# A two-layer trunk kernel on one core: five early blocks per norm, another order of steps around each way down, the float32 copy of h on VectorE

## The chip, the cores and the metric

The kernel runs on one core of a Trainium2 chip, in one launch. The metric is device time in microseconds; the lower the better. The engines are TensorE (PE in the profile), VectorE (DVE), ScalarE (ACT), GpSimd (POOL) and SyncE (SP), which issues the transfers.

## The reference, cut to what matters

The input is x, 256 tokens of 2048 features, in float32. Two layers follow each other; in each, a modulated norm feeds a mixer and a second modulated norm feeds a feed-forward block (FFN) with a short causal convolution.

```python
mod = (c_act @ ada_w[i] + ada_b[i])[:, None, :]
sh1, sc1, g1, sh2, sc2, g2 = jnp.split(mod, 6, axis=-1)
h = rms_norm(x, norm_g[i, 0]) * (1.0 + sc1) + sh1
y = even_mixer(h, ...) if i % 2 == 0 else odd_mixer(h, ...)
x = x + g1 * y
h = rms_norm(x, norm_g[i, 1]) * (1.0 + sc2) + sh2
x = x + g2 * conv_ffn(h, ffn_w_up[i], ffn_conv_w[i], ffn_conv_b[i], ffn_w_down[i])

def conv_ffn(h, w_up, conv_w, conv_b, w_down):
    u = causal_dwconv(h @ w_up, conv_w, conv_b)      # width 3, per channel
    a, b = jnp.split(u, 2, axis=-1)                  # D_FF = 5632 each
    return (jax.nn.silu(a) * b) @ w_down
```

Layer 0 has the even mixer (a convolution module and sparse attention), layer 1 the odd one (sliding-window attention and a gated block).

## The kernel before, in words

**Tiling.** x is kept transposed in `xT`, 128 features on the partitions, 16 feature tiles (kt) and 256 tokens. A *block* is 128 output features over all kt. Weights stream from memory on SP's queue into raw tiles (`Weights.load_to`, three buffers). A piece is then split (`split_to`, L123 to L141): `whi` is the rounded part, made by ACT (L133), and `wlo` the rest, made by DVE, or by POOL for a share of them (L139, POOL only when `W.hold` is off). Three products per tile, high by high, high by low and low by high, give a float32 product. `mm_t` issues them: in layer 0 as three matmuls of 256 columns (L356 to L358, *unpaired*), in layer 1's FFN as one of 512 columns and one of 256 (L349 to L353, *paired*), after which `halves` folds the bank's two halves with an ACT copy (L689) and a DVE add (L690).

**The order.** The order on each engine is written by hand: what the Python code emits first stands first. `take()` (L319) hands out the next split piece, two ahead (AHEAD), and with it runs `advance()` (L281): one step of every chain in `steps`, and the start of one chain from `waiting` (two if more than two wait). A chain is a list of small steps, for example what follows an up block: fold, convolution (`conv`: ACT L666, DVE L667 and L668), silu or `gate` (DVE L673, then ACT L678 for the high part of g and DVE L679 for its low part). `tick()` emits `ada()` at a set rate: one DVE instruction over 128x2048 (L269), 192 in all, each making one column of the modulation; not while `W.hold`. `modulation()` emits missing columns on the spot.

**The norm stage.** Three of the four norms start with `Modulated.outer(n)`: before the norm's statistics are known, the first n blocks run over raw float32 weights (L360, two records per block and kt) against `hr`, which is x times the gain, with a 257th column for the shift (ACT L484 and L485, two kt ahead; DVE L472 for the gain `gs`). FIRST = 7 blocks in each FFN, FIRST_U = 6 in layer 1's mixer. At kt == STATS all chains are drained and `token_rstd` sums the squares (PE L443); at kt == STATS + SPREAD the result is spread (PE L419, DVE L454), and from there on the 16 tiles of h are made: DVE L529, ACT L531 (float32 copy `hf`) and L532 (high part), DVE L537 (low part). During these steps ada runs at the rate ADA_O. Then `W.hold` is set, so that no ada and no POOL split falls in, until four more blocks have run.

**The FFN.** Its 44 gates go in four quarters of QK = 11. In each, 22 up blocks run, then one more of the next quarter as cover (not in the last), then 16 down blocks over the 11 tiles of g, taken as pieces of five and six kt. `W.hold` is on from the quarter's last up block. `gated(k, q)` hands out g; before the last tile, k == 10 of the first down block, it calls `drain()`, which emits all that is left of every chain at once. "Turn" below means this passage from up to down.

Of the kernel before, what the change touches and what calls it, by code (L numbers as in the profile page):

```python
# [8 lines left out]
F32 = mybir.dt.float32  # L9
F32R = mybir.dt.float32r  # L10
I32 = mybir.dt.int32
AF = mybir.ActivationFunctionType
# [10 lines left out]
KF = FF // P  # L23
NQ = 4
QK = KF // NQ
FIRST = 7
FIRST_U = 6
HEADS = 8
NC = 15
L = 32  # L30
# [18 lines left out]
PER = 4  # L49
CAP = 4.0  # L50
LEAD = 4
STATS = 3
SPREAD = 2
ADA_O = 0.7
LO_A = 0.25
ADA_A = 0.25
CONV_A = 0
# [95 lines left out]
def trunk(ctx, tc, a, out):  # L153
# [134 lines left out]
    def advance():  # L288
        for s in list(steps):
            s.pop(0)()  # L290
        steps[:] = [s for s in steps if s]
        for _ in range(1 + (len(waiting) > 2)):
            if not waiting:
                break
            s = waiting.pop(0)
            s.pop(0)()
            if s:
                steps.append(s)
# [13 lines left out]
    def hook():  # L312
        for q in (hooks, beside):
            f = q.pop(0) if q else None
            if f:
                f()


    def take():  # L319
        w = W.take()  # L320
        advance()
        hook()
        tick()
        return w

    def drain():
        while steps or waiting:
            advance()
# [128 lines left out]
    class Modulated:  # L457
# [57 lines left out]
        def begin(self):  # L515
            kt = self.n
            self.n += 1
            gs, sh = self.gain(kt)
            t = sm.tile([P, T], F32, tag="hn", name="hn")
            if self.whole:  # L520
                if kt % 4 == 0:
                    self.tiles.append(hm.tile([P, 4, T], F32, tag="hm", name="hw"))
                V.tensor_tensor(t, xT[:, kt], self.bc, op=ALU.mult)
                S.activation(self.tiles[-1][:, kt % 4], t, AF.Identity, bias=sh, scale=gs)
                return
            if kt % 2 == 0:
                self.tiles.append(hm.tile([P, 2, 2, T], F32R, tag="hm", name="h"))
            h = self.tiles[-1][:, kt % 2]
            V.tensor_tensor(t, xT[:, kt], self.bc, op=ALU.mult)  # L529
            f = sm.tile([P, T], F32, tag="hf", name="hf")  # L530
            S.activation(f, t, AF.Identity, bias=sh, scale=gs)  # L531
            S.activation(h[:, 0], t, AF.Identity, bias=sh, scale=gs)  # L532
            self.open.append((h, f))

# [119 lines left out]
    def ffn(i, rest, last, split, up, down, share, pair):  # L654
        with tc.tile_pool(name=f"ffn{i}", bufs=2) as fp:
# [2 lines left out]
            h = Modulated(i, 1)  # L658
            out_rest(i, h, *rest)
            W.share = share  # L660
            half, gt = {}, {}

            def conv(o, jj, ab):
                w = fcw[:, jj + ab * KF]
# [6 lines left out]
            def gate(jj):  # L671
                y = half.pop((jj, 0))
                V.tensor_tensor(y, y, half.pop((jj, 1)), op=ALU.mult)  # L673
                q, j = divmod(jj, QK)
                if j % 2 == 0:
                    gt[q, j // 2] = fp.tile([P, 2, 2, T], F32R, tag="g", name="g", bufs=6)
                g = gt[q, j // 2][:, j % 2]
                steps.append([lambda: S.activation(g[:, 0], y, AF.Copy),  # L678
                              lambda: V.tensor_sub(g[:, 1], y, g[:, 0].bitcast(F32))])  # L679

            def gated(k, q):
                if k == QK - 1:
                    drain()
                    W.hold = False
                return gt[q, k // 2][:, k % 2]

# [5 lines left out]
            def follow(o, jj, ab, *before):  # L692
                if o.shape[-1] == 2 * T:
                    before = *before, *halves(o)
                    o = o[:, :T]
                if ab == 0:
                    waiting.append([*before, lambda: conv(o, jj, 0), lambda: S.activation(half[jj, 0], half[jj, 0], AF.Silu)])  # L697
                else:
                    waiting.append([*before, lambda: conv(o, jj, 1), lambda: gate(jj)])
# [18 lines left out]
            for q in range(NQ):  # L718
                if q:
                    rate["ada"] = up  # L720
                for b in range(2 * QK * q + (q > 0) if q else FIRST, min(2 * QK * (q + 1) + 1, 2 * KF)):
                    if q == 0 and b == FIRST + 4:
                        W.hold = False
                    if b == 2 * QK * (q + 1) - 1:
                        W.hold = True
                    follow(proj_t(h, pair=pair), b // 2, b % 2, *[lambda: None] * (2 if b == FIRST and b % 2 else 0))
                rate["ada"] = down
                end = q == NQ - 1
                for kt in range(KD):
                    if end and kt == KD - 2:  # L730
                        rate["ada"] = 0.0
                    if end and kt == KD - 1 and not last:
                        nxt = Modulated(i + 1, 0)
                        nxt.raw(0)
                    o = proj_t(lambda k: gated(k, q), QK, pair)
                    then = []
                    if end:
                        then = [lambda kt=kt: nc.sync.dma_start(last[:, kt], xT[:, kt])] if last else square_in(kt)
                    add_into_x(o, kt, i, 5, then)
# [881 lines left out]
```

## Time and profile before

| what | value |
|---|---|
| time, median of 3 runs | 2373.77 us (2373.11 to 2376.73) |
| the profiled execution | 2380.04 us, its span 2378.3 us |
| PE busy | 2288.6 us, 96% of the span, 14056 records |
| DVE busy | 1786.0 us, 75% |
| ACT busy | 1053.7 us, 44% |
| POOL busy | 379.4 us, 16%, all in the first 22 of 40 slices |
| transfers | 596.36 MB, mean 251 GB/s |
| mean granted clock of TensorE | 0.988 of full speed |

A record of a matmul in the timeline starts before the one ahead of it has ended, since matmuls are pipelined; the pace is read from start to start. "Idle before" is what the engine waited, and the name behind the arrow what ended it.

### The profile page before, as it was taken

What the parts mean: (1) busy time and instruction counts of PE and PEld (TensorE: products, weight loads), DVE (VectorE), ACT (ScalarE), POOL (GpSimd) and SP (SyncE); (2) the same over time, 40 slices, a digit from 0 to 9 for tenths busy, and PEclk for the clock granted to TensorE, in tenths of its full rate; (3) what the DMA queues carried; (4) which work ended last, traced back from release to release, by engine and by line L of the source; (5) the groups of instructions that cost most, each with busy time, mean ns of one, the idle gap of its engine ahead of it and who ended that gap; (6) DMA issues with size and microseconds to landing.
All of it is one profiled execution on the core that took longest, in us unless ns stands there. A gap on an engine that the chain in (4) does not pass through costs nothing. (4 is left out here: it accounts for less than half of the span.)

```text
span 2378.3 us, 36086 instructions
## 1 busy us (share of the span) xinstructions
PE 2288.6 (96%) x14056; PEld 2019.1 (85%) x14056; DVE 1786.0 (75%) x2827; ACT 1053.7 (44%) x1884; POOL 379.4 (16%) x238
## 2 busy tenths in 40 slices
PE   6898999999999999999999999999999999999999
PEld 3476677889999999999999777998788888888888
DVE  7758689747968878887986877667976766766765
ACT  2021254116444544544544556447544544554553
POOL 4233435101322222222222020000000000000000
PEclk9999999999999999999999999999999999999999
DMA  9968754776878878978887853556856546545545
GB/s 383 426 231 328 307 197 174 271 264 250 321 264 334 334 283 312 335 281 314 340 301 268 310 203 115 160 171 241 324 182 210 180 157 210 181 156 203 190 150 169
DMA packets 96365, 596.36 MB, mean 251 GB/s; under 512 B 11457, under 2 KB 14145, under 8 KB 44097
## 3 DMA queue, kind: packets, MB, share of 16 engines
q1 hardware_dynamic: 96194, 594.06, 68.4%
q8 instruction: 110, 1.80, 0.3%
q14 instruction: 61, 0.50, 0.1%
HBM read 591.92 MB, written 2.10 MB: 250 GB/s over the span
## 5 line engine op out<-in xcount | busy, mean ns | idle before, releaser
L133 ACT ACTIVATE whi<-raw 128x1024 fp32r<-128x1024 f32 (+2 forms) x659 | 626.8, 952 | 775.3 <-PE bank L357 352.3
L139 DVE TENSOR_TENSOR wlo<-raw,whi 128x1024 fp32r<-128x1024 f32 (+2 forms) x586 | 660.5, 1129 | 366.1 <-ACT whi L133 365.6
L269 DVE CUSTOM_DVE_ANT_0 ada<-ada,cB,adab 128x2048 f32<-128x2048 f32 x192 | 468.9, 2445 | 26.6 <-DMA ada<-adaw 26.0
L352 PE MATMUL bank<-h,whi 128*128 128x512 f32 x1215 | 432.6, 398 | 0.0
L358 PE MATMUL bank<-h,wlo 128*128 128x256 f32 x1328 | 377.3, 284 | 5.5 <-POOL wlo L139 4.9
L356 PE MATMUL bank<-h,whi 128*128 128x256 f32 x1328 | 377.1, 284 | 0.0
L357 PE MATMUL bank<-h,whi 128*128 128x256 f32 x1328 | 376.5, 284 | 0.0
L353 PE MATMUL bank<-h,wlo 128*128 128x256 f32 x1215 | 342.8, 282 | 5.5 <-DVE wlo L139 5.5
L139 POOL TENSOR_TENSOR wlo<-raw,whi 128x1024 fp32r<-128x1024 f32 (+2 forms) x73 | 192.1, 2634 | 667.4 <-ACT whi L133 601.3
L352 PEld LDWEIGHTS bank<-h,whi 128*128 128x128 f32 x1215 | 228.3, 188 | 51.3
L358 PEld LDWEIGHTS bank<-h,wlo 128*128 128x128 f32 x1328 | 255.6, 192 | 6.8 <-POOL wlo L139 5.7
L357 PEld LDWEIGHTS bank<-h,whi 128*128 128x128 f32 x1328 | 255.7, 193 | 0.0
L356 PEld LDWEIGHTS bank<-h,whi 128*128 128x128 f32 x1328 | 255.6, 192 | 0.0
L353 PEld LDWEIGHTS bank<-h,wlo 128*128 128x128 f32 x1215 | 229.4, 189 | 15.2 <-DVE wlo L139 12.0
L352 PE MATMUL bank<-g,whi 128*128 128x512 f32 x640 | 235.2, 407 | 0.9 <-DVE g L679 0.9
L357 PE MATMUL bank<-g,whi 128*128 128x256 f32 x704 | 199.6, 284 | 0.9 <-DVE g L679 0.9
L358 PE MATMUL bank<-g,wlo 128*128 128x256 f32 x704 | 200.1, 284 | 0.3
L356 PE MATMUL bank<-g,whi 128*128 128x256 f32 x704 | 199.3, 283 | 0.8 <-ACT g L678 0.8
L353 PE MATMUL bank<-g,wlo 128*128 128x256 f32 x640 | 182.7, 285 | 0.0
L360 PE MATMUL bank<-hw,raw 128*128 128x256 f32 x640 | 150.7, 390 | 14.1 <-DMA raw<-ev 9.5
L360 PEld LDWEIGHTS bank<-hw,raw 128*128 128x128 f32 x640 | 122.0, 195 | 43.4 <-issue 20.0
L352 PEld LDWEIGHTS bank<-g,whi 128*128 128x128 f32 x640 | 123.7, 193 | 28.7 <-ACT y L697 1.2
(281 smaller groups left out, 3696.9 us busy)
## 6 DMA issues: line engine op xcount, KB each, us to landing
ada<-adaw SPq DMA_DIRECT2D x192, 1024.0 KB, 6.1
raw<-wup SPq DMA_DIRECT2D x162, 1024.0 KB, 5.8
raw<-wdn SPq DMA_DIRECT2D x128, 704.0 KB, 4.2
raw<-out SPq DMA_DIRECT2D x44, 512.0 KB, 3.9
raw<-ev_a SPq DMA_DIRECT2D x16, 1024.0 KB, 4.9
raw<-ev SPq DMA_DIRECT2D x16, 896.0 KB, 14.7
raw<-wup SPq DMA_DIRECT2D x16, 896.0 KB, 4.7
raw<-cmp_w SPq DMA_DIRECT2D x8, 1024.0 KB, 8.5
```

What stands on the lines that cost most here:

```text
L133: nc.scalar.activation(hi[:, :n], raw, AF.Copy)
L139: eng.tensor_sub(lo[:, :n], raw, hi[:, :n].bitcast(F32))
L269: V.tensor_tensor_reduce(w, w, cB, 1.0, adab[:, i * 96 + j:i * 96 + j + 1], ALU.mult, ALU.add, m)
L352: PE.matmul(o, hi[:, s_], xx, start=start, stop=False)
L353: PE.matmul(o[:, :T], lo[:, s_], x[:, 0], start=False, stop=False)
L356: PE.matmul(o, hi[:, s_], x[:, 0], start=start, stop=False)
L357: PE.matmul(o, hi[:, s_], x[:, 1], start=False, stop=False)
L358: PE.matmul(o, lo[:, s_], x[:, 0], start=False, stop=stop)
L360: PE.matmul(o, w[:, s_], x, start=start, stop=stop)
```

## The change

FIRST and FIRST_U become 5, STATS 1 and ADA_O 0.3. `take()` runs `advance()` a second time while `W.hold` is on. The float32 copy of h is made by DVE in place of ACT. At the turn, not every chain is drained: `advance()` is called until the low part of the quarter's last gate has been emitted. The quarter's last up block is unpaired in layer 1's FFN too. Lines move by two behind L321 and by up to seven behind L678.

```diff
-FIRST = 7
-FIRST_U = 6
+FIRST = 5
+FIRST_U = 5
...
-STATS = 3
+STATS = 1
 SPREAD = 2
-ADA_O = 0.7
+ADA_O = 0.3
...
         w = W.take()
         advance()
+        if W.hold:
+            advance()
         hook()
         tick()
...
             f = sm.tile([P, T], F32, tag="hf", name="hf")
-            S.activation(f, t, AF.Identity, bias=sh, scale=gs)
+            V.tensor_scalar(f, t, gs, sh, op0=ALU.mult, op1=ALU.add)
             S.activation(h[:, 0], t, AF.Identity, bias=sh, scale=gs)
...
-            half, gt = {}, {}
+            half, gt, gates = {}, {}, set()
...
-                steps.append([lambda: S.activation(g[:, 0], y, AF.Copy),
-                              lambda: V.tensor_sub(g[:, 1], y, g[:, 0].bitcast(F32))])
+
+                def low():
+                    V.tensor_sub(g[:, 1], y, g[:, 0].bitcast(F32))
+                    gates.add(jj)
+
+                steps.append([lambda: S.activation(g[:, 0], y, AF.Copy), low])
...
                 if k == QK - 1:
-                    drain()
+                    while (q + 1) * QK - 1 not in gates:
+                        advance()
                     W.hold = False
...
-                    follow(proj_t(h, pair=pair), b // 2, b % 2, *[lambda: None] * (2 if b == FIRST and b % 2 else 0))
+                    last_up = b == 2 * QK * (q + 1) - 1
+                    follow(proj_t(h, pair=pair and not last_up), b // 2, b % 2, *[lambda: None] * (2 if b == FIRST and b % 2 else 0))
```

On DVE, at a turn of layer 1's FFN with a cover block, before the change, from the last gate but one (L673); L667 and L668 are a convolution, L690 a fold, L679 the low part of g:

```order
L673 TENSOR_TENSOR y<-y 128x256
L690 TENSOR_TENSOR bank<-bank,z 128x256
L139 TENSOR_TENSOR wlo<-raw,whi 128x640
L667 SCALAR_TENSOR_TENSOR y<-bank,fcw,y 128x255
L668 SCALAR_TENSOR_TENSOR y<-bank,fcw,y 128x254
L139 TENSOR_TENSOR wlo<-raw,whi 128x768
L679 TENSOR_TENSOR g<-y,g 128x256
L690 TENSOR_TENSOR bank<-bank,z 128x256
L139 TENSOR_TENSOR wlo<-raw,whi 128x640
L667 SCALAR_TENSOR_TENSOR y<-bank,fcw,y 128x255
L668 SCALAR_TENSOR_TENSOR y<-bank,fcw,y 128x254
L139 TENSOR_TENSOR wlo<-raw,whi 128x768
```

and directly behind these rows, still before, from the last gate (L673) to the first sum into x (L553):

```order
L673 TENSOR_TENSOR y<-y 128x256
L690 TENSOR_TENSOR bank<-bank,z 128x256
L667 SCALAR_TENSOR_TENSOR y<-bank,fcw,y 128x255
L668 SCALAR_TENSOR_TENSOR y<-bank,fcw,y 128x254
L679 TENSOR_TENSOR g<-y,g 128x256
L139 TENSOR_TENSOR wlo<-raw,whi 128x640
L553 SCALAR_TENSOR_TENSOR xT<-bank,mod,xT 128x256
```

The same place after the change (L675 is the gate, L682 the low part, L697 the fold, L669 and L670 the convolution):

```order
L669 SCALAR_TENSOR_TENSOR y<-bank,fcw,y 128x255
L670 SCALAR_TENSOR_TENSOR y<-bank,fcw,y 128x254
L675 TENSOR_TENSOR y<-y 128x256
L139 TENSOR_TENSOR wlo<-raw,whi 128x768
L682 TENSOR_TENSOR g<-y,g 128x256
L139 TENSOR_TENSOR wlo<-raw,whi 128x640
L697 TENSOR_TENSOR bank<-bank,z 128x256
L139 TENSOR_TENSOR wlo<-raw,whi 128x768
L669 SCALAR_TENSOR_TENSOR y<-bank,fcw,y 128x255
L670 SCALAR_TENSOR_TENSOR y<-bank,fcw,y 128x254
L139 TENSOR_TENSOR wlo<-raw,whi 128x640
L555 SCALAR_TENSOR_TENSOR xT<-bank,mod,xT 128x256
```

Before, the last up block's convolution stood behind the third of the down blocks' pieces (640, 768, 640), and its low part behind the fourth and the cover block's fold and convolution. Now the convolution stands behind the first piece, the low part behind the second, and the cover block's fold and convolution come after it.

On DVE, the end of layer 0's FFN norm stage before the change, the last three tiles of h made ahead of the first split piece (L472 is the gain, L529 and L537 the steps of h):

```order
L472 SCALAR_TENSOR_TENSOR gs<-mod,normg 128x1
L529 TENSOR_TENSOR hn<-xT,bc 128x256
L537 TENSOR_TENSOR h<-hf,h 128x256
L529 TENSOR_TENSOR hn<-xT,bc 128x256
L537 TENSOR_TENSOR h<-hf,h 128x256
L472 SCALAR_TENSOR_TENSOR gs<-mod,normg 128x1
L529 TENSOR_TENSOR hn<-xT,bc 128x256
L537 TENSOR_TENSOR h<-hf,h 128x256
L139 TENSOR_TENSOR wlo<-raw,whi 128x1024
```

and after it (L533 is the float32 copy on DVE, L531 and L539 the other two steps of h, L474 the gain, L269 ada):

```order
L474 SCALAR_TENSOR_TENSOR gs<-mod,normg 128x1
L531 TENSOR_TENSOR hn<-xT,bc 128x256
L533 TENSOR_SCALAR hf<-hn,gs,mod 128x256
L539 TENSOR_TENSOR h<-hf,h 128x256
L269 ISA ada,mod<-ada,cB,adab 128x2048
L269 ISA mod 128x1
L269 ISA ada,mod<-ada,cB,adab 128x2048
L269 ISA mod 128x1
L474 SCALAR_TENSOR_TENSOR gs<-mod,normg 128x1
L531 TENSOR_TENSOR hn<-xT,bc 128x256
L533 TENSOR_SCALAR hf<-hn,gs,mod 128x256
L539 TENSOR_TENSOR h<-hf,h 128x256
```

Four ada columns fall in this stage in both, but at the lower rate two of them are still missing when the last gain (L474) needs them, and are now emitted on the spot directly ahead of it. In layer 1's mixer three columns fall in the stage where five did, in layer 1's FFN two where four did; the rest moves into the up blocks that follow.

## Rows read from the trace of the kernel before

**Rows 1.** Waits of PE, whole span: in total us, times, longest us.

```profile
engine line waited for: us in total, times, longest us
...
PE bank L349 <- ACT g L678: 7.1, 4, 2.2
...
PE bank L353 <- DVE wlo L139: 5.5, 14, 1.0
...
PE bank L358 <- POOL wlo L139: 4.9, 4, 2.3
...
PE bank L350 <- DVE g L679: 2.0, 3, 0.7
...
PE bank L360 <- ACT hr L485: 1.6, 2, 1.1
...
PE bank L357 <- DVE mix L339: 1.4, 2, 0.7
...
PE bank L357 <- DVE g L679: 0.9, 3, 0.3
...
PE bank L356 <- ACT g L678: 0.8, 1, 0.8
```

**Rows 2.** Chain that ended last, by time, layer 1's FFN norm stage: start, us.

```profile
1590.22 9.10 PE bank L360 x42
...
1606.28 33.37 PE bank L360 x154
```

**Rows 3.** Timeline of PE in up blocks: start, us, form, [idle before <-releaser].

```profile
602.32 0.28 PE L358 MATMUL bank<-h,wlo 128*128 128x256 f32 x1
...
607.36 0.28 PE L358 MATMUL bank<-h,wlo 128*128 128x256 f32 x1
...
1760.00 0.40 PE L352 MATMUL bank<-g,whi 128*128 128x512 f32 x1
...
1762.12 0.28 PE L349 MATMUL bank<-g,wlo 128*128 128x256 f32 x1
```

**Rows 4.** Timeline of PE at the first down turn of layer 1's FFN.

```profile
1742.21 0.28 PE L353 MATMUL bank<-g,wlo 128*128 128x256 f32 x1
...
1744.11 0.38 PE L349 MATMUL bank<-g,wlo 128*128 128x256 f32 x1 [1.62 <-ACT g L678]
...
1745.17 0.63 PE L350 MATMUL bank<-g,whi 128*128 128x512 f32 x1 [0.68 <-DVE g L679]
```

**Rows 5.** Timeline of PE at the last turn of layer 1's FFN.

```profile
2308.45 0.28 PE L353 MATMUL bank<-g,wlo 128*128 128x256 f32 x1
...
2309.62 0.47 PE L352 MATMUL bank<-g,whi 128*128 128x512 f32 x1 [0.89 <-DVE g L679]
...
2309.92 0.28 PE L353 MATMUL bank<-g,wlo 128*128 128x256 f32 x1
...
2312.41 0.58 PE L349 MATMUL bank<-g,wlo 128*128 128x256 f32 x1 [2.21 <-ACT g L678]
```

**Rows 6.** Windows: length, busy us of PE, PEld, DVE, ACT, POOL, clock, DMA, GB/s.

```profile
1745.40:1748.80 3.40, 3.40 (x12) 2.81 (x12) 2.20 (x3) 0.74 (x1) 0.00 (x0) 0.50 0.04 14
...
2127.70:2131.10 3.40, 3.40 (x12) 2.92 (x12) 1.92 (x3) 1.01 (x2) 0.00 (x0) 0.50 0.02 5
...
2312.00:2318.80 6.80, 6.39 (x19) 5.36 (x20) 2.89 (x5) 1.93 (x3) 0.00 (x0) 0.50 0.03 11
...
1640.00:1742.00 102.00, 96.50 (x529) 79.66 (x529) 98.17 (x153) 62.20 (x105) 0.00 (x0) 1.00 0.76 275
```

**Rows 7.** Timeline of PE in layer 1's first norm stage.

```profile
1327.02 8.17 PE L360 MATMUL bank<-hr,raw 128*128 128x257 f32 x36 [1.11 <-ACT hr L485]
...
1335.66 4.60 PE L360 MATMUL bank<-hr,raw 128*128 128x257 f32 x20 [0.47 <-ACT hr L485]
```

**Rows 8.** DVE groups by form: count, busy us, mean ns, idle before.

```profile
L269 DVE CUSTOM_DVE_ANT_0 ada<-ada,cB,adab 128x2048 f32<-128x2048 f32 x192 | 468.9, 2445 | 26.6 <-DMA ada<-adaw 26.0
...
L673 DVE TENSOR_TENSOR y<-y 128x256 f32<-128x256 f32 x88 | 38.8, 441 | 0.0
...
L529 DVE TENSOR_TENSOR hn<-xT,bc 128x256 f32<-128x256 f32 x48 | 19.8, 419 | 0.1
...
L888 DVE TENSOR_SCALAR hs<-hs 30x256 f32<-30x256 f32 x2 | 0.8, 394 | 9.1 <-ACT hs L887 9.1
...
L954 DVE TENSOR_SCALAR cy<-xp,cvw 128x256 f32<-128x256 f32 x8 | 4.5, 560 | 0.1
```

**Rows 9.** Timelines of DVE and POOL, layer 0's first up blocks.

```profile
588.78 2.63 DVE L673 TENSOR_TENSOR y<-y 128x256 f32<-128x256 f32 x1
...
587.96 3.16 POOL L139 TENSOR_TENSOR wlo<-raw,whi 128x1024 fp32r<-128x1024 f32 x1 [25.49 <-ACT whi L133]
```

**Rows 10.** Timeline of DVE in layer 1's FFN norm stage.

```profile
1591.84 0.96 DVE L433 TENSOR_TENSOR sq<-sq 128x256 f32<-128x256 f32 x2 [0.63 <-ACT sq L429]
...
1599.70 0.16 DVE L445 TENSOR_SCALAR rv<-bank 128x2 f32<-128x2 f32 x1 [6.83 <-PE bank L443]
...
1602.08 0.48 DVE L418 TENSOR_SCALAR diag<-ident,rsy 128x128 f32<-128x128 f32 x2
```

## Prediction

> **What bounds the kernel now.** I read the page's busy shares first: PE is busy 96% of the span, so PE's own work, its waits and its clock are nearly all there is. Then the waits of PE [rows 1]: most of what is left after the start of the kernel stands at the turns of the FFNs (the waits for g) and where DVE or POOL have not split a weight in time (wlo). Then the chain that ended last, in a norm stage [rows 2]: it is PE over raw weights without a gap. Then PE's timeline at a turn [rows 4, 5] and the windows behind it [rows 6]: a turn costs twice, once as a wait and once as a spell at a granted clock of 0.50 (1.2 GHz in place of 2.4) that follows it. The sum is made against the profiled execution (2380.04 us, 6.3 above the median); the difference is put on the median, 2373.8. A measurement here can tell about 0.2%, or 4.7 us, from no change.
>
> **PE's own work.** A raw record takes 9.10/42 = 217 ns, so a block costs 434 ns per kt [rows 2]. Unpaired split work costs 5.04/14 = 360 ns per kt, paired work 2.12/6 = 353 ns [rows 3]. Blocks that move from raw to split therefore save 74 or 81 ns in each of 16 kt: two in layer 0's FFN (2.4 us), one in layer 1's mixer (1.2), two in layer 1's FFN (2.6), 6.2 together. Four last up blocks that become unpaired in layer 1 cost 4 x 16 x 7 ns = 0.5. Term A: **-5.7 us**, with hardly any doubt.
>
> **The turns.** In layer 1's FFN the first turn goes from 1742.21 to 1744.11 and on to 1745.17, where 0.12 us each would be the pace: 1.78 + 0.94 = 2.72 lost [rows 4]. Then comes a spell of 3.40 us at clock 0.50, which costs half of it, 1.7 [rows 6]. The waits count three such turns: four for the high part of g, 7.1 with a last one of 2.2 that is another place, three for the low part, 2.0 [rows 1]; the third has the same spell [rows 6]. 3 x 4.42 = 13.3. The last turn, without a cover block, loses 1.05 + 2.37 [rows 5] and a spell of 6.80 at 0.50, so 3.4 more [rows 6]: 6.8. What the change does there: with two steps per take under `W.hold` the last gate's chain is emitted over half as many pieces, it no longer lies behind the cover block's fold and convolution on DVE, and the unpaired last block needs no fold. The order shows the low part moved three positions of pieces forward. It now sits about one whole cover block ahead of its use, 16 x 353 ns = 5.6 us, against a lateness of 2.7; I take the three covered turns as free. The last turn has no cover; layer 0's last turn shows what an unpaired block leaves there, 0.8 for the high part [rows 1], and I leave 0.6 of it, without a spell. In layer 0 three waits of 0.3 and that one of 0.8 [rows 1] fall to 0 and 0.6, 1.1 gained (unpaired, no spell). Term B: -13.3 - 6.8 + 0.6 - 1.1 = **-20.6**. Ends: all waits stay half (+10), or the last turn is free too (-1.2). Late next at a turn is wlo of the second down piece, which the doubled steps now push behind a convolution (0.9 us of DVE): one of it is hidden by the two pieces split ahead.
>
> **The norm stages.** Three things change: PE's cover shrinks, DVE gets f, and ada moves.
> Statistics: in layer 1's FFN the squares are complete at 1592.80 [rows 10], 2.58 us after the raw work began at 1590.22 [rows 2]. Before, 3 kt of 7 blocks (9.1 us) covered that, now 1 kt of 5 blocks, 2.17. So 0.4 is lost there; from PE's sums to the diagonal it takes 1599.70 to 1602.56, 2.9 us [rows 10], against two kt of 4.34: no wait.
> Float32 copy: the trace has no such instruction on DVE. A one-source operation with scalars took 394 ns (30x256) and 560 (128x256, beside a busy POOL) [rows 8]; these are my ends, and I take the middle, 0.48. ACT gets 16 x 0.4 us back per norm, worth nothing, as it is not waited for there. The Trainium skill (VectorE: DVE Perf Modes, section "The perf-mode tier table") has this operation at twice the rate for float32 out of SBUF, 1227 ns for 2048 elements; as an estimate from that figure some 0.29 us for 256. By it the sum would be 3 us lower in layer 0's norm. The rows above speak against it, as none of the one-source rows of 256 is that short.
> DVE's load from the spread of the statistics to the end of the stage: 16 tiles x (0.42 + 0.42 + 0.48) = 21.1 us, plus ada at 2.45 [rows 8]; PE's time for it is 13 kt x 5 x 0.434 = 28.2 (before, 11 x 7 x 0.434 = 33.4, with 13.4 + 4 x 2.45).
> Layer 0's FFN: 21.1 + 4 x 2.45 = 30.9, so 2.7 too long (1.3 to 4.0 with f at its ends). Two of these ada are emitted on the spot just ahead of the last gain, one kt of 2.17 us before `hr` needs it; it shows as a wait for hr and then for the first split pieces. Behind it the two raw blocks fewer are made up by split ones, with POOL taking a share: one more wait like the four of 1.2 on average [rows 1]. One spell at half clock, 1.7 as at a turn. Together +5.6, ends 0 and 8.3 (4.0 + two POOL waits + 1.7).
> Layer 1's mixer: 21.1 + 3 x 2.45 = 28.5, level with 28.2. The two waits for hr there, 1.6 [rows 1, 7], come with ada in between and go, as two ada leave the stage. The third split block in place of the sixth raw one also covers one wait for mix, 0.7 [rows 1]: -2.3 (ends -2.3 and +1).
> Layer 1's FFN: 21.1 + 2 x 2.45 = 26.0, room enough. But in the up blocks behind it DVE is the bound: 98.17 of 102.00 us busy, PE 96.50 [rows 6], the 14 waits of 5.5 for wlo [rows 1]. Two more split blocks add 11.3 to PE and 4 x 1.2 to DVE, two more ada 4.9. Both get 10 to 11, so the waits stay about as they are. I take -1.0 for the convolutions that are spread over more PE time, +0.4 from above: -0.6, ends -4 (DVE catches up) and +3 (all ada in the way).
> Term C: +5.6 - 2.3 - 0.6 = **+2.7**.
>
> **Sum.** -5.7 - 20.6 + 2.7 = -23.6; 2373.8 - 23.6 = **2350**.
>
> **Rivals.**
> *The norms stay free.* DVE runs ahead of PE more than its load says, since it waits little before: layer 0's norm costs 0, layer 1's FFN gains 2, the turns are all free: -5.7 - 21.2 - 2.3 - 2 = -31.2, so 2342.6. For it speaks that DVE is idle at the end of the stages; against it the two ada on the spot.
> *The turn's wait only moves.* The doubled steps crowd DVE and ACT ahead of the down pieces' wlo, so that PE waits some 1.0 us for weights at each covered turn, with the spell of 1.7, and the last turn keeps half: the turns of layer 1 then give 3 x 1.7 + 3.4 = 8.5 in place of 19.5, so 2361. For it: the same DVE work is only put in another order, and spells follow such waits. Against it: two pieces are split ahead, and no other wait lies at the turns now.
> *DVE becomes the bound in all three norms.* It decides where f takes over (28.2 - 4.9)/16 - 0.84 = 0.62 us. At 0.85, DVE falls 16 x 0.23 = 3.7 behind in each, PE stalls in most kt, and spells as after the last turn follow twice (6.8 at half, 3.4 each): 10.5 per norm, 31.5 in all, with the gain in the mixer's norm gone. -5.7 - 20.6 + 31.5 = +5.2, so 2379, slower. For it: a DVE instruction with two SBUF sources (L673, 0.44 us on average, [rows 8]) took 2.63 us while POOL split a weight from 587.96 on for 3.16 [rows 9]; f beside POOL could do the same. Against it: POOL splits nothing in these stages and is idle in layer 1. The Trainium skill (SBUF — State Buffer, section "Who interferes with whom") says that such a VectorE instruction, or one in a two-port mode, and GpSimd lock each other out for a whole instruction; the trace agrees with its 2.63 us.
> *The change does not do what it says:* the order shows each part in place, so this has no chance of its own.
>
> **How the numbers follow.** Forecast 0.53 (2344 to 2357), norms free 0.2, wait moves 0.22, DVE bound 0.03, none of these 0.02. The range 2339 to 2363 holds the first three nearly whole with their unknown costs. Faster by over 0.2% (under 2369.0): all of the first two, most of the third: 0.93; the same 0.04; slower 0.03.
>
> **What would show it.** In the changed profile the waits for g in layer 1's FFN are gone but for the last quarter, and the windows behind the three covered turns have clock 1.00. PE's busy time falls by 5.7 and by the spells, some 13 us in all. In layer 0's norm stage there is a wait for hr or wlo of one to three microseconds, behind two ada in a row. f takes 0.39 to 0.56 us. Wrong it would be if the waits for wlo grow by over 5 us at the turns, or if PE waits for h or hr in layer 1's norms.

## The result and the profile after

The changed kernel takes 2349.71 us (median of 4 runs, 2348.95 to 2351.11), the kernel before 2374.27 on the same occasion: a ratio of 0.9887, 95% interval 0.9875 to 0.9899. That is 26.9 us less by the ratio, 24.6 by the medians; forecast were 2350 and a gain of 23.6. The profiled execution took 2349.61 us.

The page's span and busy times:

```profile
span 2347.9 us, 36331 instructions
...
PE 2266.1 (97%) x14168; PEld 2007.7 (86%) x14168; DVE 1810.3 (77%) x2872; ACT 1043.4 (44%) x1840; POOL 383.2 (16%) x239
```

PE is busy 22.5 us less than in the first trace of before, and 14.8 less than in the second (2280.9; first experiment). Within their spans the clock stood at 0.50 for 56.1 and 39.2 us in those two, and for 23.9 here. Half of the differences, 16.1 and 7.7, is what half clock costs; it leaves 6.4 and 7.1 for saved work, near the 5.7 of the sum. The "some 13 us in all" of the prediction is near the fall against the second trace, and well short of that against the first.

The waits of PE, in total us, times and longest, the lines that answer to [rows 1]:

```profile
PE bank L355 <- DVE wlo L139: 4.5, 11, 1.1
...
PE bank L360 <- POOL wlo L139: 4.5, 8, 0.9
...
PE bank L360 <- DVE wlo L139: 2.1, 3, 1.0
...
PE bank L358 <- ACT whi L133: 0.6, 1, 0.6
...
PE bank L362 <- ACT hr L487: 0.5, 1, 0.5
...
PE bank L352 <- DVE g L682: 0.4, 1, 0.4
...
PE bank L359 <- DVE g L682: 0.4, 1, 0.4
```

The waits for g are down from 11.7 us (7.1 + 2.0 + 0.9 + 0.8, and the 0.89 of [rows 5]) to 0.8, those for hr from 1.6 to 0.5. Those for split weights stay: before, wlo cost 4.9 from POOL and 0.5 from DVE in unpaired blocks and 5.5 in paired ones, now 4.5 + 2.1 and 4.5; a wait for whi of 0.6 is new.

PE's timeline at the first turn of layer 1's FFN, the place of [rows 4]:

```profile
1729.51 0.28 PE L355 MATMUL bank<-g,wlo 128*128 128x256 f32 x1
1729.63 0.28 PE L351 MATMUL bank<-g,wlo 128*128 128x256 f32 x1
1729.75 0.40 PE L352 MATMUL bank<-g,whi 128*128 128x512 f32 x1
```

No gap is left where 1.62 and 0.68 us stood. And at the last turn, the place of [rows 5]:

```profile
2284.20 0.28 PE L355 MATMUL bank<-g,wlo 128*128 128x256 f32 x1
2284.61 0.39 PE L351 MATMUL bank<-g,wlo 128*128 128x256 f32 x1
2285.36 0.51 PE L352 MATMUL bank<-g,whi 128*128 128x512 f32 x1 [0.37 <-DVE g L682]
```

From 2284.20 to 2285.36 there are 1.16 us for two steps of 0.12: 0.9 is lost, where it was 3.4. Windows behind the first, the second, the third and the last turn (length, then busy us of PE, PEld, DVE, ACT, POOL, the clock, the DMA share, GB/s):

```profile
1736.80:1740.20 3.40, 3.40 (x20) 2.99 (x21) 3.17 (x6) 0.74 (x1) 0.00 (x0) 1.00 0.69 225
...
1917.20:1920.60 3.40, 3.40 (x21) 2.93 (x20) 2.19 (x6) 1.82 (x3) 0.00 (x0) 1.00 0.58 210
2103.60:2107.00 3.40, 3.40 (x21) 2.93 (x20) 2.19 (x6) 1.83 (x3) 0.00 (x0) 1.00 0.56 210
2285.60:2289.00 3.40, 3.40 (x20) 2.97 (x20) 1.75 (x3) 1.59 (x2) 0.00 (x0) 1.00 0.62 217
```

The clock is 1.00 in all four; before, it was 0.50 behind the first, the third and the last [rows 6].

Where the time went is best read by stretches, from the start of PE's first record of one stage to that of the next, in its timeline. The up blocks and the ways down come out the same within 0.2 us from trace to trace unless a spell at half clock falls into them, and so does layer 1's FFN norm (145.5 to 145.7 in three traces of the same code), so they tell more than a kernel's whole time. The other stretches vary more, with no edit in them: the start took 508.7 to 516.1 us over all traces of this document, layer 1's mixer 286.5 to 290.3 in six traces of the same code, layer 0's FFN norm 144.8, 146.2 and 146.0 in three. One trace can't tell a difference of 2 us there. The kernel before was profiled a second time (first experiment), and the table has both.

| stretch | before | before, again | after |
|---|---|---|---|
| start to layer 0's FFN norm | 513.0 | 512.3 | 512.2 |
| layer 0's FFN norm to its first way down | 146.7 | 145.9 | 144.8 |
| its four ways down (each up to the next up block or norm) | 258.5 | 258.5 | 257.2 |
| its other up blocks | 378.0 | 377.9 | 377.9 |
| layer 1's mixer, norm and all | 293.8 | 293.3 | 288.1 |
| layer 1's FFN norm to its first way down | 148.7 | 148.4 | 145.5 |
| its first three ways down | 199.2 | 197.7 | 187.7 |
| its other up blocks | 367.4 | 367.3 | 367.6 |
| its last way down and the end | 72.9 | 71.8 | 67.0 |

The end of layer 0's norm stage is where the sum expected the change to cost. DVE and, below it, POOL in the changed kernel:

```profile
540.96 2.35 DVE L269 CUSTOM_DVE_ANT_0 ada<-ada,cB,adab 128x2048 f32<-128x2048 f32 x1
...
543.23 2.35 DVE L269 CUSTOM_DVE_ANT_0 ada<-ada,cB,adab 128x2048 f32<-128x2048 f32 x1
...
545.50 0.16 DVE L474 SCALAR_TENSOR_TENSOR gs<-mod,normg 128x1 f32<-128x1 f32 x1
...
548.80 2.06 DVE L139 TENSOR_TENSOR wlo<-raw,whi 128x1024 fp32r<-128x1024 f32 x1 [2.02 <-ACT whi L133]
```

```profile
547.40 2.37 POOL L139 TENSOR_TENSOR wlo<-raw,whi 128x1024 fp32r<-128x1024 f32 x1 [118.32 <-ACT whi L133]
```

Two ada stand ahead of the last gain, as the order showed; then DVE's first weight split takes 2.06 us, 1.2 being usual, beside POOL's, which started first and ended at 549.77: from there on it took 1.1. On PE this comes to five short waits, none with a spell behind it:

```profile
546.43 2.43 PE L362 MATMUL bank<-hr,raw 128*128 128x257 f32 x10 [0.53 <-ACT hr L487]
...
549.83 0.39 PE L360 MATMUL bank<-h,wlo 128*128 128x256 f32 x1 [0.73 <-POOL wlo L139]
...
560.09 0.38 PE L360 MATMUL bank<-h,wlo 128*128 128x256 f32 x1 [1.02 <-DVE wlo L139]
...
563.60 0.39 PE L358 MATMUL bank<-h,whi 128*128 128x256 f32 x1 [0.62 <-ACT whi L133]
...
564.86 0.39 PE L360 MATMUL bank<-h,wlo 128*128 128x256 f32 x1 [0.76 <-DVE wlo L139]
```

The float32 copy on DVE takes 0.413 us each (count, busy us, mean ns, idle before):

```profile
L533 DVE TENSOR_SCALAR hf<-hn,gs,mod 128x256 f32<-128x256 f32 x48 | 19.8, 413 | 1.7
```

### The profile page after: what moved, and what is told of

Same layout as the page of the kernel before. It is cut to its first block, busy times and chain, and to the rows that moved or that the text cites. A ratio compares the mean times of both kernels' runs of the same rounds, so it can differ in the third digit from the quotient of the medians.

```text
span 2347.9 us, 36331 instructions
## 1 busy us (share of the span) xinstructions
PE 2266.1 (97%) x14168; PEld 2007.7 (86%) x14168; DVE 1810.3 (77%) x2872; ACT 1043.4 (44%) x1840; POOL 383.2 (16%) x239
## 3 DMA queue, kind: packets, MB, share of 16 engines
q1 hardware_dynamic: 96914, 594.06, 68.6%
## 4 chain that ended last, share of the span: by engine, by line
PE 77%; DVE 13%; DMA 5%; issue 2%; ACT 2%; POOL 2%; SPq 0%; DVEq 0%; ACTq 0%; POOLq 0%
PE bank L354 15%; PE bank L360 11%; PE bank L359 11%; PE bank L358 11%; PE bank L362 10%; PE bank L355 8%; DVE ada L269 4%; DMA raw<-ev 2%; DVE wlo L139 2%; PE bank L373 1%; PE bank L370 1%; PE bank L371 1%; PE bank L369 1%; PE bank L352 1%; POOL wlo L139 1%
## 5 line engine op out<-in xcount | busy, mean ns | idle before, releaser
L133 ACT ACTIVATE whi<-raw 128x1024 fp32r<-128x1024 f32 (+2 forms) x669 | 637.1, 953 | 763.9 <-PE bank L359 357.9
L139 DVE TENSOR_TENSOR wlo<-raw,whi 128x1024 fp32r<-128x1024 f32 (+2 forms) x595 | 674.1, 1135 | 355.6 <-ACT whi L133 350.6
L269 DVE CUSTOM_DVE_ANT_0 ada<-ada,cB,adab 128x2048 f32<-128x2048 f32 x192 | 476.7, 2486 | 27.2 <-DMA ada<-adaw 26.4
L354 PE MATMUL bank<-h,whi 128*128 128x512 f32 x1185 | 421.9, 398 | 0.8 <-ACT whi L133 0.8
L360 PE MATMUL bank<-h,wlo 128*128 128x256 f32 x1440 | 408.4, 284 | 5.5 <-POOL wlo L139 3.4
L358 PE MATMUL bank<-h,whi 128*128 128x256 f32 x1440 | 408.1, 283 | 0.6 <-ACT whi L133 0.6
L359 PE MATMUL bank<-h,whi 128*128 128x256 f32 x1440 | 407.4, 283 | 0.0
L355 PE MATMUL bank<-h,wlo 128*128 128x256 f32 x1185 | 333.8, 282 | 3.6 <-DVE wlo L139 3.5
L360 PEld LDWEIGHTS bank<-h,wlo 128*128 128x128 f32 x1440 | 276.3, 192 | 7.2 <-POOL wlo L139 4.2
L358 PEld LDWEIGHTS bank<-h,whi 128*128 128x128 f32 x1440 | 276.3, 192 | 0.9 <-ACT whi L133 0.8
L359 PEld LDWEIGHTS bank<-h,whi 128*128 128x128 f32 x1440 | 276.3, 192 | 0.2
L354 PEld LDWEIGHTS bank<-h,whi 128*128 128x128 f32 x1185 | 222.6, 188 | 51.4 <-ACT whi L133 1.1
L355 PEld LDWEIGHTS bank<-h,wlo 128*128 128x128 f32 x1185 | 223.7, 189 | 11.2 <-DVE wlo L139 7.7
L354 PE MATMUL bank<-g,whi 128*128 128x512 f32 x640 | 228.6, 398 | 0.0
L358 PE MATMUL bank<-g,whi 128*128 128x256 f32 x704 | 199.2, 283 | 0.0
## 6 DMA issues: line engine op xcount, KB each, us to landing
raw<-ev SPq DMA_DIRECT2D x16, 896.0 KB, 14.7
```

What stands on the lines that cost most here:

```text
L133: nc.scalar.activation(hi[:, :n], raw, AF.Copy)
L139: eng.tensor_sub(lo[:, :n], raw, hi[:, :n].bitcast(F32))
L269: V.tensor_tensor_reduce(w, w, cB, 1.0, adab[:, i * 96 + j:i * 96 + j + 1], ALU.mult, ALU.add, m)
L354: PE.matmul(o, hi[:, s_], xx, start=start, stop=False)
L355: PE.matmul(o[:, :T], lo[:, s_], x[:, 0], start=False, stop=False)
L358: PE.matmul(o, hi[:, s_], x[:, 0], start=start, stop=False)
```

## The experiments

Each kernel was profiled; where a median with an interval is given it was also timed against the kernel before. Stretches are those of the table.

**The kernel before, once more** (no edit).

> The kernel before, profiled once more. If the 6.3 us by which the first profiled execution stood over the median were chance of that one execution, this one stands within 3 us of 2374, and the stretches of the two traces show in which part of the program the difference lies. If the profile itself costs those 6 us, this one comes out near 2380 again.

It took 2374.75, with a span of 2373.0. So the first execution was long by chance, and the place of most of it is seen: 0.7 in the stretch up to layer 0's FFN norm, 0.8 in that norm's stretch, 1.5 and 1.1 at the last two turns of layer 1's FFN. PE at the third of them, and windows behind the first and the third:

```profile
2122.90 0.38 PE L349 MATMUL bank<-g,wlo 128*128 128x256 f32 x1 [1.62 <-ACT g L678]
...
2123.97 0.50 PE L350 MATMUL bank<-g,whi 128*128 128x512 f32 x1 [0.68 <-DVE g L679]
```

```profile
1743.00:1746.40 3.40, 3.40 (x13) 2.83 (x11) 2.39 (x3) 1.14 (x2) 0.00 (x0) 0.55 0.06 22
...
2124.30:2127.70 3.40, 3.40 (x20) 2.94 (x19) 1.88 (x3) 1.59 (x2) 0.00 (x0) 1.00 0.07 23
```

The waits before it are the same 1.62 and 0.68 us as at the first turn, but the clock behind is 1.00 here, and 0.50 at the same place in the first trace [rows 6]. A wait of this size does not always bring a spell.

**The part for the turns alone**, in the kernel before:

```diff
         advance()
+        if W.hold:
+            advance()
...
-                    drain()
+                    while (q + 1) * QK - 1 not in gates:
+                        advance()
...
-                    follow(proj_t(h, pair=pair), ...
+                    follow(proj_t(h, pair=pair and not last_up), ...
```

> The kernel before with the part for the turns alone (two steps per take under hold, only the last gate waited for, last up block unpaired). Theory (the turns give nearly all of the gain): term B and the unpaired blocks, -20.6 + 0.5, so about 2354, and no spell at half clock behind the three covered turns of layer 1's FFN. Rival (the turn's wait only moves, and the norms gave the rest): 2362 to 2366, with new waits for wlo at the turns.

2362.09 us against 2376.16, ratio 0.9941 [0.9929, 0.9954]: a gain of 14 us, between the theory's 20 and the rival's 8 to 12. The turns did what the theory says: ways down of layer 1's FFN of 63.6, 62.1, 62.1 and 67.3 us, no spell behind them, no wait for g left but 0.37 at the last; at the first, 0.23 and 0.70 for wlo. But the stretches ahead of the first ways down grew to 148.1 us in layer 0 and 150.4 in layer 1. Some 1.7 of each is spells (6.8 us at half clock in layer 0's, where before had 3.4, and 3.4 in layer 1's, where before had none), and PE has new waits there (in total us, times, longest):

```profile
PE bank L354 <- ACT whi L133: 1.8, 1, 1.8
...
PE bank L358 <- ACT whi L133: 1.5, 1, 1.5
```

**The norms alone**, in the kernel before:

```diff
-FIRST = 7
-FIRST_U = 6
-STATS = 3
-ADA_O = 0.7
+FIRST = 5
+FIRST_U = 5
+STATS = 1
+ADA_O = 0.3
```

> The kernel before with five early blocks, STATS 1 and ADA_O 0.3 alone; the float32 copy stays on ScalarE. Theory (PE's saved work comes through, and VectorE has room without the copy): -6.2 of PE work, -2.3 in layer 1's mixer, -1 in layer 1's FFN, +1.5 for the two ada on the spot in layer 0: 2366. Rival (ScalarE, with the copy on it, can't keep up over the shorter stage): waits for h, hr or whi at the end of each norm stage, 3 us or more each, so 2372 or slower.

2369.87 us, ratio 0.9975 [0.9966, 0.9985]: 6 us, some 2 short of the theory's 8. Layer 1 took 289.2 and 146.6 us in its mixer and in its FFN's first stretch, 6.3 less than before where the theory has 7.1. Layer 0's stretch took 149.7, 3 more than before, with two spells of 3.4 us at half clock where before had one. It has a wait for whi from ACT, as the rival says, and one of 2.0 us for wlo, at the place of the 2.3 of [rows 1]:

```profile
PE bank L358 <- DVE wlo L139: 2.7, 2, 2.0
...
PE bank L356 <- ACT whi L133: 1.6, 1, 1.6
```

**The copy alone**, in the kernel before:

```diff
-            S.activation(f, t, AF.Identity, bias=sh, scale=gs)
+            V.tensor_scalar(f, t, gs, sh, op0=ALU.mult, op1=ALU.add)
```

> The kernel before with the float32 copy of h on VectorE alone. Theory (seven raw blocks cover it: VectorE's load with the copy at 0.41 us is 29.8 us against 33.4): no difference, 2372 to 2376. Rival (ScalarE was what ended the norm stages late, and the copy's move frees it): 1 to 4 us faster, 2370 to 2373, with the waits for hr in layer 1's mixer gone.

2376.28 against 2376.16, ratio 1.0 [0.9991, 1.0009]: nothing, as the theory has it. By stretches it is two things that offset each other: layer 0's got 1.4 longer than the mean of before (147.8, in this trace without a spell), layer 1's 2.0 shorter (146.5). So even with seven blocks the copy's place matters in layer 1's FFN norm; it is the whole that comes to nothing. The three parts apart come to 14 + 6 + 0 = 20 us; the whole gave 26.9 by its ratio.

**The change with the copy back on ACT** (the last diff, the other way round).

> The changed kernel with the float32 copy of h back on ScalarE. The parts measured apart (turns 14, norms 6, copy 0) add to less than the whole (about 26). Theory (the copy's move is worth something only with five blocks: ScalarE, with hr, whi and two copies of h to make, is what the shorter norm stage of layer 0 waits for): 4 to 6 us slower than the changed kernel, nearly all of it between the start of layer 0's norm stage and its first way down (144.8 us in the changed kernel, about 149.5 here). Rival of the prediction (VectorE is the one short of time there, so the copy costs): 1 to 3 us faster than the changed kernel.

2357.21 us, ratio 0.9924 [0.9912, 0.9937], against 0.9887 for the change: 7.5 us slower by the medians, 8.8 by the ratios. So the copy's move is worth nothing on the whole with seven blocks and about a third of the gain with five. By stretches, layer 0's took 147.0 (144.8), the mixer 289.8 (288.1), layer 1's 148.9 (145.5). The theory had nearly all of it in layer 0; only layer 1's 3.4 is clear of what the same code gives from trace to trace, and 1.7 of it is a spell at half clock. The waits of PE for hr, whi and wlo grew by 4.4 us in all, among them:

```profile
PE bank L355 <- DVE wlo L139: 5.9, 12, 1.1
...
PE bank L358 <- ACT whi L133: 1.5, 2, 0.8
...
PE bank L362 <- ACT hr L487: 0.8, 1, 0.8
```

That ACT is what is late shows on DVE, in layer 1's FFN norm. The first two weight splits, each behind a wait for ACT's whi, with the copy back on ACT:

```profile
1619.17 1.23 DVE L139 TENSOR_TENSOR wlo<-raw,whi 128x1024 fp32r<-128x1024 f32 x1 [5.90 <-ACT whi L133]
...
1622.91 1.22 DVE L139 TENSOR_TENSOR wlo<-raw,whi 128x1024 fp32r<-128x1024 f32 x1 [1.84 <-ACT whi L133]
```

and in the change:

```profile
1614.79 1.23 DVE L139 TENSOR_TENSOR wlo<-raw,whi 128x1024 fp32r<-128x1024 f32 x1 [5.26 <-ACT whi L133]
...
1618.05 1.23 DVE L139 TENSOR_TENSOR wlo<-raw,whi 128x1024 fp32r<-128x1024 f32 x1 [0.92 <-ACT whi L133]
```

From the start of the stage (1583.4 and 1580.0) these are 35.8 and 39.5 us against 34.8 and 38.0: 1.0 and 1.5 later.

The rival, by which the copy costs on DVE, was the prediction's own step, and it falls. Turns and norms without the copy's move give 18 us together, 20 apart; what was missing in the sum of the parts is what the copy's move is worth beside them.

**The second step at the turns only:**

```diff
-        if W.hold:
+        if W.turn:
             advance()
```

with `W.turn` set and cleared with `W.hold` at the turns, but not behind a norm.

> The changed kernel with the second step per take at the turns alone, no longer in the first four up blocks behind a norm. Theory (the doubled steps there push convolutions ahead of the weight splits on VectorE and ScalarE, and cost about 1.3 us in layer 0's FFN and 2 in layer 1's): the two stretches from a norm to the first way down get 1 to 2 us shorter each, 2346 to 2348 against 2349.7. Rival (those waits come from the norm stages' backlog itself, and slower chains only move it back): no difference, or slower by up to 2 us.

2349.60 us, ratio 0.9891 [0.9876, 0.9907]: no difference. Layer 0's stretch was 146.7 with a spell in it, layer 1's 145.5. The rival holds, and the trace shows how slower chains move the waits back:

```profile
599.65 0.58 PE L360 MATMUL bank<-h,wlo 128*128 128x256 f32 x1 [2.36 <-DVE wlo L139]
```

This wait, with the spell behind it, stands where the kernel before had its 2.3 for wlo [rows 1]. All seven traces with one step per take behind the norm have one of 1.8 to 2.4 us there (before twice, the norms alone, the copy alone, this one, and two below); the six with two steps and five or more blocks have none, but in most of them more early waits. So the doubled steps behind a norm trade one late wait for several early ones.

**One step per take everywhere** (the second `advance()` of the change removed), and **every chain drained at the turn** (`drain()` in place of the loop over gates, two steps kept).

> The changed kernel with one step per take everywhere. It tells what the second step does at the turns beside waiting for the last gate alone. Theory (both are needed, since the last gate's chain starts only as the pieces are taken): the covered ways down of layer 1's FFN take 64 to 66.4 us (62.1 with two steps, 66.4 before), the last 69 or more (67.0). Rival (the narrower wait alone does it): 62.1 and 67.0.

> The changed kernel with every chain drained at the turn again, two steps per take kept. Theory (with two steps the last gate is done early enough, and the drain adds only the cover block's convolution, which stands behind it): covered ways down of layer 1's FFN 62.1 to 62.8 us. Rival (the cover block's fold and convolution ahead of the last gate were what made it late): 64 us or more.

These two were profiled only (2354.69 and 2347.39 us), so by stretches: the second and third ways down of layer 1's FFN take 62.6 and 62.5 us with one step, 62.1 with the drain, against 66.4 before; the last one 68.6 and 67.1 (67.0). With the drain every way down is as in the change: beside two steps and the unpaired block, the narrower wait adds nothing. The 2347.39 is 2.3 below the change, but its stretch up to layer 0's FFN norm, which the edit doesn't touch, was 3.5 shorter. With one step the theory, 64 us or more for the covered turns, falls.

**Only the unpaired last up block** (both undone), and **only the other two** (that block paired again).

> The changed kernel with one step per take and every chain drained at the turn, so that of the part for the turns only the unpaired last up block is left. Either of the other two alone gave 62.1 to 62.6 us per covered way down of layer 1's FFN. Theory (the unpaired block is what makes the turn, by leaving out a fold): 62.5 to 63 us here too, and about 69 for the last. Rival (the three are in place of each other only in part, and the cover block's chain is in the way when neither of the two is there): 64 to 66.4 us.

> The changed kernel with the last up block of a quarter paired again. Theory (the doubled steps and the narrower wait make the covered turns without it, and it matters only where no cover block runs): covered ways down 62.1 to 62.5 us, the last 68 to 69.5 in place of 67.0. Rival (the fold is what makes the last gate late): 64 us or more, with a spell at half clock behind them.

These were profiled only, too. The unpaired block alone: 64.0, 62.6, 62.6 and 68.6 us. The other two without it: 64.1, 62.1, 62.1 and 70.0, where PE waits at the last turn and a spell follows. (The 64.0 and 64.1 hold a wait for wlo of 1.20 and 1.45 us behind the first turn; the change has 0.71 there.)

```profile
2294.34 0.38 PE L351 MATMUL bank<-g,wlo 128*128 128x256 f32 x1 [1.86 <-ACT g L685]
```

So the unpaired block alone removes the covered turns' waits but for 0.26 us each, and the doubled steps with the narrower wait remove them without it; neither of those two was run alone. At the last turn, without a cover block, the unpaired block and the doubled steps add up: 71.8 to 72.9 before, 68.6 with the unpaired block, 67.0 with the doubled steps beside it. The narrower wait made no difference in either pair that tells it apart: 67.0 and 67.1 with two steps, 68.6 and 68.6 with one. The whole time of the paired kernel, 2360.49, has 3.9 us in the stretch up to layer 0's FFN norm (516.1 against 512.2) which its edit doesn't touch.

**ADA_O at 0.7 again**, in the change.

> The changed kernel with ADA_O at 0.7 again. Theory (the two ada on the spot ahead of the last gain are worth the wait for hr of 0.5 us and little more in layer 0, and in layer 1 the lower rate is what took the waits for hr out of the mixer's stage): layer 0's stretch from the norm's start to the first way down 144 to 145 us (144.8), layer 1's mixer stage 1 to 3 us longer than the 35.6 us. Rival (the lower rate does harm alone, by bunching the columns): layer 0's stretch 3 us shorter, layer 1's the same.

The rival falls, and of the theory only the mixer's waits for hr hold, at over twice the size. It took 2365.43 us (one execution), 16 more than the change, and PE waited 13 times for hr:

```profile
PE bank L362 <- ACT hr L487: 13.2, 13, 2.2
```

Layer 0's stretch was 148.7 us (144.8), the mixer 296.9 (288.1), layer 1's 149.2 (145.5); the three norm stages themselves took 41.8, 43.0 and 42.5 us (36.3, 35.6 and 36.1). DVE shows how, at the end of layer 0's stage: an ada, then what it holds up, the gain; and PE, below, waiting for the hr made with that gain:

```profile
536.52 2.34 DVE L269 CUSTOM_DVE_ANT_0 ada<-ada,cB,adab 128x2048 f32<-128x2048 f32 x1
...
539.91 0.15 DVE L474 SCALAR_TENSOR_TENSOR gs<-mod,normg 128x1 f32<-128x1 f32 x1
```

```profile
537.38 2.43 PE L362 MATMUL bank<-hr,raw 128*128 128x257 f32 x10 [1.02 <-ACT hr L487]
...
540.84 4.60 PE L362 MATMUL bank<-hr,raw 128*128 128x257 f32 x20 [1.03 <-ACT hr L487]
```

An ada of 2.34 us and the three steps of one tile of h, about 1.1, stand between two gains, together 3.4, and PE's cover for one kt of five blocks is 2.17: with no lead left on DVE, an ada shows at once as a wait of 1.0 to 1.2 us. An ada in the stage doesn't cost that by itself: in the change three fall in the mixer's stage and two in layer 1's FFN's, without a wait for hr. What decides is how many there are. Here six fall in each stage, where the change has four, three and two. By the prediction's own sum for DVE that is 16 x (0.42 + 0.42 + 0.41) + 6 x 2.45 = 34.7 us against the 28.2 that PE gives, 6.5 too long, and the stages grew by 5.5, 7.4 and 6.4. The smaller rate isn't an extra of the change but what lets five blocks be enough.

**Four early blocks per norm**, in the change:

```diff
-FIRST = 5
-FIRST_U = 5
+FIRST = 4
+FIRST_U = 4
```

(and the raw pieces cut by kt as before).

> The changed kernel with four early blocks per norm in place of five. Theory (VectorE now ends the norm stages: 13 kt of four blocks are 22.6 us, against 16 x 3 x 0.42 = 20.2 for the tiles of h and 5 to 10 for ada): the 3.7 us of PE work saved (three blocks more that are split) are more than eaten by waits for h and wlo of 2 to 5 us per norm: 2351 to 2358. Rival (VectorE's backlog hides in the split up blocks behind): 2346 to 2348.

2366.27 us, ratio 0.9966 [0.9952, 0.9979]: 16.6 slower than the change, more than the theory's 2 to 8. The waits for hr and for wlo from DVE are back:

```profile
PE bank L362 <- ACT hr L487: 9.5, 11, 3.2
...
PE bank L360 <- DVE wlo L139: 3.8, 4, 2.1
```

The first stretch of layer 0's FFN took 153.2, that of layer 1's 151.6, the mixer 292.2. The sum for DVE has the signs right here too: with the four, three and two ada of the change's rate it is 7.2, 4.8 and 2.3 over PE's 13 x 4 x 0.434 = 22.6, and the stages took 36.1, 33.6 and 32.6 us, 8.3, 5.8 and 4.8 more than the bare 27.8. No version tried beats the change by more than a measurement can tell.

## Why the prediction was right, and where it was off

The range was met by the turns, which the prediction had right in kind; that the total came within 1 us was luck, since three errors offset each other. By terms, measured as the changed kernel's stretches less the mean of the two traces of before (the first and the third row rest on stretches that vary by 1.4 and 3.8 us with the same code, the others on steady ones):

| term | forecast | measured |
|---|---|---|
| layer 0's FFN norm (-2.4 of work, +5.6) | +3.2 | -1.5 |
| layer 0's turns | -1.1 | -1.3 |
| layer 1's mixer (-1.2 of work, -2.3) | -3.5 | -5.5 |
| layer 1's FFN norm (-2.6 of work, -0.6, +0.1) | -3.1 | -3.1 |
| layer 1's turns | -19.5 | -16.1 |
| the rest | +0.4 | -0.2 |
| sum | -23.6 | -27.7 |

**PE's own work** came through as far as it can be told: 6.4 and 7.1 us are left of the fall in busy time when half clock is taken out, where 5.7 was forecast. The stages of five blocks take 36.3, 35.6 and 36.1 us where 16 x 5 x 0.434 = 34.7 is the bare work. The paired pace in the sum was read from rows of a down block ([rows 3] name g), not of up blocks; the up blocks have it too, 22 of them in 124.3 us from 1805.15 on in the kernel before, 353 ns per kt.

**Layer 1's turns** did what was forecast, with the waits of 2.72 gone and the clock at 1.00. They gave 3.4 less. Some 0.7 of it is "the third has the same spell": each of the three was charged 1.7, and in the second trace of before the third had none. Some 0.9 is the last turn, where the spell was 6.8 us in the first trace and 3.4 in the second. The largest part, 1.4, is the first way down (63.5 against 62.1), which kept waits of 0.24 and 0.71 us for wlo: once the hold is off, an ada comes ahead of a down piece's wlo on DVE, here at 1733.45, and PE waits for it at 1736.72:

```profile
1733.45 2.34 DVE L269 CUSTOM_DVE_ANT_0 ada<-ada,cB,adab 128x2048 f32<-128x2048 f32 x1
1735.71 0.95 DVE L139 TENSOR_TENSOR wlo<-raw,whi 128x768 fp32r<-128x768 f32 x1
```

```profile
1736.72 0.38 PE L355 MATMUL bank<-g,wlo 128*128 128x256 f32 x1 [0.71 <-DVE wlo L139]
```

The prediction had named wlo of the second down piece as late next, and taken it as hidden. It was partly right on the last turn, 0.6 forecast to be left and 0.9 found, without a spell as it said.

**The float32 copy** was priced rightly, 0.48 in the sum between ends of 0.39 and 0.56, 0.413 measured, while the estimate from the Trainium skill's table, 0.29, does not hold in this kernel. But its sign in the sum was wrong. "DVE 2.7 too long" did show as the wait for hr and the first split pieces that were named, 0.53, 0.73 and 1.02 us. What the step left out is ACT: with the copy on it, ACT is late with whi behind the short stage, by 1.0 and 1.5 us for the first two pieces of layer 1's FFN. The runs put the copy's move at some 8 us for the three norms (0.9924 against 0.9887); the stretches of one trace each show 7.3 of it, of which 4.4 is seen as waits and 1.7 as a spell. "Worth nothing, as it is not waited for there" was read from stages of seven and six blocks and did not hold for five; in layer 1's FFN it did not hold for seven either (146.5 against 148.5).

**Layer 0's norm** is the term that failed by most, +5.6 against about +0.9 (+2.1 by the two other traces of the same code; its upper end of 8.3 adds up to 8.1). Besides the copy, it counted the new waits and not the old one in the same stretch: the 2.3 us for POOL's wlo in [rows 1], with a spell behind it (the clock was 0.85 and 0.81 in the two windows of 5 us from 595 on), which are gone after the change. The runs above put that down to the doubled steps behind the norm, which the prediction weighed at the turns only. The five new waits add to 3.7 and bring no spell, where one of 1.7 had been charged.

**Layer 1's mixer** gained 2.0 more than forecast in this trace; over six traces of the same code it gained 1.4 more, within their spread. The waits for hr and one for mix went as named; one of 0.9 for wlo right behind the norm stage went too in this trace, and it had not been counted. In others of the six, waits of up to 0.8 are there.

**The rivals.** That the norms stay free was close to what the profile showed in layer 0, and 2342.6 was too low since the turns gave less. That the turn's wait only moves came true at the first covered turn alone, with 0.71 us for wlo and no spell; the second and third have no wait at all, and the clock is 1.00 behind all three. That DVE becomes the bound in all three norms is not what the change does, but the mechanism is real: with the old ada rate it costs 16 us, and with four blocks as much. The load over the stage that the prediction summed up is what tells it, and ada was the term to watch. The rival's point of 0.62 us for the copy was worked out for two ada in a stage; with the six of the old rate the same sum gives (28.2 - 14.7)/16 - 0.84 = 0.00, so a copy of any length makes PE wait. Its counter-argument was wrong in two places, without effect on the sum: POOL does split one piece at the end of layer 0's norm stage (547.40 above, at 560.11 in the kernel before), and it isn't idle in all of layer 1, since it works in the 24th of the 40 slices, in the mixer, beside the first 22.

## What to carry to other kernels

When a cover is shortened, sum up all that the helping engines must do under it, background work included, and compare the sum with what is left of the cover: a rate of background work that was harmless before can cost most of the gain after, and the sum told its size. A move of work between two helper engines can come to nothing in the old schedule and to a third of the gain in the new one, so price it in the changed schedule, on the engine that is freed as well as on the one that is loaded. When a stretch is re-planned, count the waits that are already in it: they can go with the old plan. And before a difference of a stretch is explained, see how much the same code varies there.

## What the runs showed that was not expected

The same wait before the same work is followed by a spell at half clock in one execution and not in another: 1.62 and 0.68 us at the third turn of layer 1's FFN, then a clock of 0.50 in the first trace of before and 1.00 in the second. Two of the twelve covered turns in the four traces with the old turn had none. Such a spell costs 1.5 to 1.7 us. The first trace of before has 13 spells in its span and the second 10, so they can by themselves make its spread, 2370.42 to 2379.38 us over the timed runs of before; that was not shown run by run.

DVE's split of a weight took 2.06 us instead of 1.2 beside one on POOL that had started 1.4 us earlier, and ended 1.1 after it. The prediction had such a lock only among a rival's reasons, at another place.
